# Second unit's token and query loads placed behind a GpSimd copy of the first scores' maxima

## The chip, the cores and the metric
The kernel runs on one core of a Trainium2 chip. The metric is device microseconds of one execution, as the median of three; a profile of one further execution shows what each engine did. The engines are PE (TensorE, matrix products), DVE (VectorE), ACT (ScalarE), POOL (GpSimd) and SP (SyncE). SP issues DMA transfers on the hardware queue q1, POOL issues them on the software queue q0; both are served by the same 16 DMA engines.

## The reference
One layer: RMSNorm, one input projection, two groups of four heads side by side, an output projection with a residual, then a mixture of experts with a residual. All inputs are float32, 2048 tokens of width 1024.

```python
h    = rms_norm(x)
proj = h @ w_in            # mLSTM q,k | v | o | i | f  and attention q | k | v
# group A, 4 heads: mLSTM memory; q, k through a causal conv of 4 taps and SiLU
b    = cumsum(log_sigmoid(f));  m_t = max(b + m, max_s(b_t - b_s + i_s))
hm   = (q k^T * exp(log_d - m_t)) v + exp(b + m - m_t) * q C,  divided by its norm
# group B, 4 heads, two 64-wide q/k maps c = 0, 1 each, q and k RMS-normed
p_c  = softmax(mask(q_c k_c^T / 8))          # chunk-causal, queries in blocks of 128
ha   = (p_0 - lambda * p_1) v
y    = x + concat(rms(sigmoid(o) * hm), rms(ha)) @ w_out
out  = y + moe(rms_norm(y))                  # top 1 of 4 groups, top 2 of 8 experts
```

The softmax subtracts the row's maximum; `nm` in the kernel is that maximum times -1/8, one column for each of the two maps.

## The kernel before
**Stages.** First the projection runs over pairs of 128-token blocks. It writes the normed tokens (`hT_d`), and attention's queries, keys and values (`q_d`, `k_d`, `v_d`), to DRAM; attention's q and k stand in two tiles `qkT` on the chip, from which the stores go out (L355). The group projected last holds the tokens that the next stage needs first. For these, eight loads (L348 on SP for queries, L349 on POOL for keys) copy q and k straight out of `qkT` into a tile `R`, without the way over DRAM.

Then come the heads, r = 0 to 3, each over 16 blocks g of 128 tokens; two blocks are a unit U of 256 tokens. For a unit the kernel needs its tokens `hs` (two loads of 1 MB from `hT_d`, L478; even units use `hs0`, odd ones `hs1`) and its queries `qt` (four loads of 128 KB, L487); for every four blocks it needs keys `kt` (L497, POOL) and values `va` (L499, SP). For unit 0 `hs0` is already on chip, and `qt` and part of `kt` are cast from `R` (L408, L409).

Of each block it computes: scores of both maps against all keys so far (L586, and L589 for the mask), their maxima `mx` (L590) and `nm` (L598), the exponential `prob` (L601, ACT), the combined probabilities (L618), their transposes (L632) and products with the values (L645); and of the mLSTM the values and output gate (vo, L94 to L96), the q and k of a unit (qk, L514 to L516, then the convolution at L531), a decay matrix `vb` (loaded at L671 from `vrow_d`, mask added on POOL at L672), and the products at L691 and L692.

**The passage between the two stages.** The gates of all tokens are computed once, in four pieces (lines 402 to 463): `gates_a` transposes the gate columns, casts `qt` and `kt` of unit 0 out of `R`, and runs two scans on DVE (`g_bc` at L420, `g_gm` at L421) over `g_lf`; `gates_b` transposes their last columns on PE (L427) and runs short scans in `g_mr` (L430 to L434); `gates_c` brings the result back through PE (L438) and makes `vrow`, which SP stores (L445); `gates_d` makes four tables. The pieces stand between the first block's matmuls, in this order of the program:

```python
load_kv(0); load_hs(1); load_qt(1)
gates_a(); vo_atoms(0); qk_atoms(0, 0); gates_b(); qk_atoms(0, 1)
gates_c(); score_atoms(0); vo_atoms(1); gates_d(0..3); combine_atoms(0)
```

**What sets the order.** The text of the program gives the work; a scheduler with estimates of its own orders the instructions of each engine and gives each tile its place in memory, taking up memory that earlier tiles have left. An instruction that writes such a place waits for those that read it before. Every engine, and each engine's DMA issues, run in their order, so an instruction that waits holds all behind it on that engine. `after(later, earlier)` keeps two instructions in order; `mark` holds instructions for it.

The lines below are those of the kernel before; in the changed kernel lines 495 to 740 stand 7 further down, so that L514 is L521 there.

Of the kernel before, what the change touches and what calls it, by code (L numbers as in the profile page):

```python
# [7 lines left out]
F32 = mybir.dt.float32  # L8
# [11 lines left out]
P = 128  # L20
# [40 lines left out]
def block_kernel(tc, a, out):  # L61
    nc = tc.nc
    V, A, G, T = nc.vector, nc.scalar, nc.gpsimd, nc.tensor
# [29 lines left out]
    def mm3(ps, xh, xl, wh, wl, start, stop):  # L93
        T.matmul(ps, xh, wh, start=start, stop=False)  # L94
        T.matmul(ps, xh, wl, start=False, stop=False)  # L95
        T.matmul(ps, xl, wh, start=False, stop=stop)  # L96
# [9 lines left out]
    with tc.tile_pool(name="const", bufs=1) as cp, tc.tile_pool(name="dram", bufs=1, space=DRAM) as dp:  # L106

        hT_d = dp.tile([NB, P, 2, DC, P], F32, name="hT_d")
        q_d = dp.tile([H, 4, 2, 2, 64, 512], F32, name="q_d")
# [47 lines left out]
        mark = {}  # L157

        def after(later, earlier):

            tc.add_manual_dep(later.ins, earlier.ins.name,
                              mybir.DependencyInfo(mybir.DependencyClass.NoSync, mybir.DependencyReason.DATA),
                              reason="issue order")
# [79 lines left out]
        with tc.tile_pool(name="wa", bufs=1) as wap, tc.tile_pool(name="sa", bufs=2) as sx, \  # L243
# [33 lines left out]
            with tc.tile_pool(name="wst", bufs=4, reuse_waits="tile") as sp:  # L277
                for j, (dst, src, n) in enumerate(pieces):
                    k = 2 if n > 4 else DC
                    for d in range(0, DC, k):  # L280
# [4 lines left out]
                        ld = nc.sync.dma_start(st, w_in[d * P:(d + k) * P, src:src + n].rearrange("(c p) n -> p c n", p=P))  # L285
# [9 lines left out]
            sp = sa2.__enter__()  # L295

            for p in range(NB):
                i, b = order[p], p % 2
# [83 lines left out]
        sp = rr.__enter__()  # L382
# [53 lines left out]
        def gates_c():  # L436
            pt = small(HC, 1)
            T.matmul(pt, gt["mp"], ones64[:1, :1], start=True, stop=True)  # L438
            mprev = g_tile("mprev", HC, 1)
            V.tensor_copy(mprev, pt)  # L440
            mt, ur, ir, em = gt["f"], gt["t1"], gt["lf"], gt["zr"]
            gt.update(ur=ur, ir=ir, em=em, dg=gt["gm"][:, :HC])
            V.scalar_tensor_tensor(mt, gt["bc"], mprev, gt["gm"], op0=OP.add, op1=OP.max)
            V.tensor_tensor(vrow, gt["bc"], mt, OP.subtract)
            nc.sync.dma_start(vrow_d, vrow)  # L445
            V.tensor_tensor(ur, gt["i"], gt["bc"], OP.subtract)
            A.activation(ir, vrow, AF.Exp, bias=mprev)
            V.tensor_scalar(em, mt, -1.0, math.log(4.0 * math.sqrt(128.0)), op0=OP.mult, op1=OP.add)
            A.activation(em, em, AF.Exp)
            V.tensor_scalar(gt["dg"], ident[:HC, :HC], ir[:, P - 1:P], None, op0=OP.mult)  # L450
# [14 lines left out]
        W, HS, QT, KT, VA, SIL, BLK, UN, CST = {}, {}, {}, {}, {}, {}, {}, {}, {}  # L465
        raw_prev = {}

        def w_of(r, k):
            j = r % 2 * 2 + k
            return (H4[j].rearrange("p (d n) -> p d n", d=DC), L4[j].rearrange("p (d n) -> p d n", d=DC))  # L470

        def load_hs(U):
            if U >= 32:
                return
            u = U % 8
            HS[U] = sp.tile([P, 2, 2, DC, P], F32R, name="hs1", bufs=1) if U % 2 else hs0
            for b in range(2):
                G.dma_start(HS[U][:, b], hT_d[2 * u + b])  # L478

        def load_qt(U):  # L480
            if U >= 32:
                return
            r, u = divmod(U, 8)
            QT[U] = sp.tile([P, 2, 2, 256], F32R, name="qt")
            for hl in range(2):
                for o in range(2):
                    G.dma_start(QT[U][hl * 64:(hl + 1) * 64, o],  # L487
                                q_d[r, u // 2, hl ^ o, :, :, u % 2 * 256:(u % 2 + 1) * 256].rearrange("m d t -> d m t"))

        def load_kv(B):  # L490
            if B >= 16:
                return
            r, sb = divmod(B, 4)
            KT[B] = sp.tile([P, 2, 512], F32R, name="kt", bufs=5)
            t0 = 0 if B else 256
            for hl in range(2):
                G.dma_start(KT[B][hl * 64:(hl + 1) * 64, :, t0:], k_d[r, sb, hl, :, :, t0:].rearrange("m d t -> d m t"))  # L497
            VA[B] = sp.tile([P, 4, HD], F32, name="va", bufs=5)
            nc.sync.dma_start(VA[B], v_d[sb * 512:(sb + 1) * 512, r * P:(r + 1) * P].rearrange("(b p) e -> p b e", p=P))  # L499
# [37 lines left out]
        def unit(U):  # L537
            if U not in UN:
                UN[U] = {n: sp.tile([P, 2, HD + x], F32, name=n) for n, x in (("mst", 0), ("ast", 0), ("num", 1), ("tho", 0))}
                UN[U]["nrm"] = sp.tile([P, 4], F32, name="nrm")  # L540
            return UN[U]

        def vo_atoms(g):
            r, i = divmod(g, NB)
            U, b = g // 2, g % 2
            box = {}

            def mms(d0):
                wh, wl = w_of(r, 1)
                if d0 == 0:  # L550
                    box["ps"] = pp.tile([P, 512], F32, name="w", bufs=3)
                ps = box["ps"][:, :256]
                for d in (d0, d0 + 1):
                    mm3(ps, HS[U][:, b, 0, d, :], HS[U][:, b, 1, d, :], wh[:, d, :], wl[:, d, :], d == 0, d == DC - 1)
                if d0 == DC - 2:
                    v1 = sp.tile([P, HD + 1], F32, name="v1")
                    G.memset(v1[:, HD:], 1.0)
                    v_ = A.activation(v1[:, :HD], ps[:, :HD], AF.Copy)
                    if g == 0:
                        after(v_, mark["LN"])  # L560
                    A.activation(unit(U)["tho"][:, b, :], ps[:, HD:], AF.Tanh, scale=0.5)
                    BLK.setdefault(g, {})["v1"] = v1
            return [lambda d0=d0: mms(d0) for d0 in (0, 2, 4, 6)]

        def score_atoms(g):
            r, i = divmod(g, NB)
            sb, b = divmod(i, 4)
            nch = sb + 1
            B = BLK.setdefault(g, {})
            width = [512 if c < sb else (b + 1) * P for c in range(nch)]  # L570

            def score(m, c):
                if m == 0 and c == 0:
                    B["mx"] = sp.tile([P, 2, 4], F32, name="mx")
                    B["nm"] = sp.tile([P, 2], F32, name="nm")
                    B["rs"] = sp.tile([P, 2, 4], F32, name="rs")
                    B["rt"] = sp.tile([P, 2], F32, name="rt")
                    B["rv"] = sp.tile([P, 2], F32, name="rv", bufs=3)
                    B["cc"] = sp.tile([P, 1], F32, name="cc")
                if c == 0:  # L580
                    B["p", m] = sp.tile([P, S], F32, name="prob", bufs=3)
                n = width[c]
                ps = pp.tile([P, 512], F32, name="sc", bufs=5)
                B["sc", m, c] = ps
                for o in range(2):
                    T.matmul(ps[:, :n], QT[g // 2][:, o, m, g % 2 * P:(g % 2 + 1) * P], KT[r * 4 + c][:, m, :n],  # L586
                             start=o == 0, stop=o == 1 and c < sb)
                if c == sb:
                    T.matmul(ps[:, n - P:n], qm, km, start=False, stop=True)  # L589
                V.reduce_max(B["mx"][:, m, c:c + 1], ps[:, :n], axis=AX.X)  # L590
                if c < nch - 1:
                    return
                mx, nm = B["mx"], B["nm"][:, m:m + 1]
                src = mx[:, m, 0:1]
                if nch > 1:
                    V.reduce_max(nm, mx[:, m, :nch], axis=AX.X)
                    src = nm
                V.tensor_scalar(nm, src, -0.125, None, op0=OP.mult)  # L598
                for c2 in range(nch):
                    n = width[c2]  # L600
                    mark["ACT"] = A.activation(B["p", m][:, c2 * 512:c2 * 512 + n], B["sc", m, c2][:, :n], AF.Exp, bias=nm,  # L601
                                 scale=0.125, accum_out=B["rs"][:, m, c2:c2 + 1])
            return [lambda m=m, c=c: score(m, c) for m in range(2) for c in range(nch)]
# [133 lines left out]
        HS[0] = hs0  # L737
        QT[0] = sp.tile([P, 2, 2, 256], F32R, name="qt")
        load_kv(0)
        load_hs(1)  # L740
        load_qt(1)
        def run(fs):
            for f in fs:
                f()
# [5 lines left out]
        run(qk_atoms(0, 1))  # L750
        gates_c()
        run(score_atoms(0))
        run(vo_atoms(1))
        for j in range(4):
            gates_d(j)
# [36 lines left out]
        for g in range(NS):  # L792
            r, i = divmod(g, NB)
            U = g // 2
# [84 lines left out]
        def first_half(e):  # L879

            return 12 * e - 4 if e else 0
# [301 lines left out]
        with tc.tile_pool(name="mo", bufs=2, reuse_waits="tile") as sp, \  # L1183
# [159 lines left out]
            for e in range(NE + 1):  # L1343
                u = first_half(e)
# [136 lines left out]
```

## Time and profile before

| | |
|---|---|
| median of 3 runs | 2171.48 us (2170.26 to 2174.47) |
| profiled execution | 2174.06 us, its span 2172.2 us |
| PE busy | 2046.9 us, 94% of the span |
| DVE / ACT / POOL busy | 1604.7 (74%) / 1231.4 (57%) / 516.6 (24%) us |
| DMA traffic | 449.79 MB, 207 GB/s over the span |
| mean granted clock of PE | 0.981 of full speed |

The projection ends at 327.5 us, the heads' stage starts there. Times in the rows are microseconds from the start of the span. A row of a timeline gives start, duration, engine, line, operation, the tile written and those read, and in brackets how long the engine idled before it and what ended that. [...] DMA rows give the size of one transfer and the time from issue to landing.

### The profile page before, as it was taken

The numbers are of one execution on the slowest core, as the hardware profiler recorded it, in microseconds if no ns is written. First come the engines' busy times: TensorE is split into PE (matmuls) and PEld (weight loads), VectorE is DVE, ScalarE is ACT, GpSimd is POOL, SyncE is SP. The second block draws the span as 40 slices with busy tenths as digits, with TensorE's granted clock in tenths as the row PEclk, the third lists the DMA queues.
The fourth block names the chain that finished last, engine by engine and source line by source line (L and its number), as shares of the span: only waits on it lengthen the run. The fifth ranks groups of instructions, "written<-read, shape, count | busy, mean of one in ns | idle before, by whom it ended". The sixth has DMA issues, their size and how long they took to land. (4 is left out here: it accounts for less than half of the span.)

```text
span 2172.2 us, 40513 instructions
## 1 busy us (share of the span) xinstructions
PE 2046.9 (94%) x13815; PEld 1734.3 (80%) x13816; DVE 1604.7 (74%) x4375; ACT 1231.4 (57%) x2820; POOL 516.6 (24%) x685
## 2 busy tenths in 40 slices
PE   7999997999999999999999999598999999999987
PEld 6888886899999899999987888476777666766765
DVE  7667655788687778878877777787878656786863
ACT  5344334666566566656663233477777656667764
POOL 4000003223322322232201111313232332223322
PEclk9999998999999999999999999799999999999999
DMA  7555438645663645375417844499999768898983
GB/s 231 177 173 171 160 102 249 167 123 134 190 159 107 175 140 159 89 200 162 122 51 258 271 146 137 145 330 303 363 348 347 243 228 295 301 334 285 352 280 75
DMA packets 241654, 449.79 MB, mean 207 GB/s; under 512 B 36432, under 2 KB 120720, under 8 KB 231376
## 3 DMA queue, kind: packets, MB, share of 16 engines
q1 hardware_dynamic: 192736, 317.08, 43.2%
q0 software_dynamic: 48352, 127.93, 21.6%
q8 instruction: 161, 2.64, 0.5%
q14 instruction: 133, 1.09, 0.2%
q10 hardware_dynamic: 272, 1.05, 0.1%
HBM read 377.72 MB, written 84.25 MB: 213 GB/s over the span
## 5 line engine op out<-in xcount | busy, mean ns | idle before, releaser
L70 DVE TENSOR_TENSOR L<-R,H 128x1024 fp32r<-128x1024 f32 x408 | 485.6, 1222 | 126.9 <-ACT H L66 117.1
L66 ACT ACTIVATE H<-R 128x1024 fp32r<-128x1024 f32 x408 | 415.8, 1056 | 30.7 <-DVE cnti L1174 9.2
L1247 PE MATMUL pgu<-H,xT 128*128 128x512 f32 x1024 | 359.9, 410 | 15.4 <-issue 6.6
L1247 PEld LDWEIGHTS pgu<-H,xT 128*128 128x128 f32 x1024 | 196.1, 191 | 58.0 <-issue 16.9
L601 ACT ACTIVATE prob<-sc,nm 128x512 f32<-128x512 f32 (+3 forms) x320 | 195.8, 623 | 50.8 <-DVE nm L598 44.4
L590 DVE TENSOR_REDUCE mx<-sc 128x1 f32<-128x512 f32 (+3 forms) x320 | 186.8, 602 | 24.2 <-PE sc L586 14.5
L1247 PE MATMUL pgu<-L,xT 128*128 128x512 f32 x512 | 203.2, 397 | 1.4 <-DVE L L70 1.4
L586 PE MATMUL sc<-kt,qt 128*128 128x512 f32 (+3 forms) x640 | 189.6, 386 | 2.0 <-ACT prob L601 1.8
L1262 PE MATMUL py<-H,hT 128*128 128x512 f32 x512 | 175.3, 405 | 11.0 <-issue 9.5
L94 PE MATMUL w<-H,hs 128*128 128x256 f32 x512 | 156.2, 305 | 5.8 <-DVE num L706 5.0
L645 PE MATMUL w<-va,aT 128*128 128x128 f32 x1088 | 155.6, 277 | 5.9 <-ACT raw L524 4.4
L514 PE MATMUL w<-hs,H 128*128 128x256 f32 x512 | 158.1, 309 | 1.7 <-ACT aT L636 0.9
L645 PEld LDWEIGHTS w<-va,aT 128*128 128x128 f32 x1088 | 139.3, 191 | 11.2 <-ACT raw L524 6.5
L515 PE MATMUL w<-hs,H 128*128 128x256 f32 x512 | 145.0, 283 | 0.0
L95 PE MATMUL w<-L,hs 128*128 128x256 f32 x512 | 145.0, 283 | 0.0
L516 PE MATMUL w<-hs,L 128*128 128x256 f32 x512 | 144.9, 283 | 0.0
L96 PE MATMUL w<-H,hs 128*128 128x256 f32 x512 | 144.9, 283 | 0.0
L1262 PEld LDWEIGHTS py<-H,hT 128*128 128x128 f32 x512 | 97.1, 190 | 43.7 <-issue 21.8
L1247 PEld LDWEIGHTS pgu<-L,xT 128*128 128x128 f32 x512 | 98.5, 192 | 18.3 <-DVE L L70 1.7
L1209 POOL DMA_INDIRECT xg<-h_d,ix x64 | 89.7, 1401 | 97.3 <-PE pt L1220 47.1
L1324 POOL TENSOR_SCALAR yE<-yE,ix 32x1024 f32<-32x1024 f32 (+1 forms) x20 | 57.0, 2852 | 231.4 <-ACT yE L1323 223.2
L1271 POOL DMA_INDIRECT out<-y,ix x32 | 57.5, 1795 | 226.5 <-ACT y L1267 125.4
(377 smaller groups left out, 5254.1 us busy)
## 6 DMA issues: line engine op xcount, KB each, us to landing
R<-w_gate SPq DMA_DIRECT2D x128, 512.0 KB, 10.8
R<-w_up SPq DMA_DIRECT2D x128, 512.0 KB, 11.9
R<-w_down SPq DMA_DIRECT2D x63, 1024.0 KB, 11.0
hs<-hT_d POOLq DMA_DIRECT2D x62, 1024.0 KB, 5.3
hT_d<-hs SPq DMA_DIRECT2D x16, 1024.0 KB, 4.0
qt<-q_d POOLq DMA_DIRECT2D x124, 128.0 KB, 6.3
xt<-x SPq DMA_DIRECT2D x30, 512.0 KB, 4.4
q_d<-qkT SPq DMA_DIRECT2D x32, 256.0 KB, 3.7
```

The lines of the kernel that those rows point to most:

```text
L66: return A.activation(dst, src, AF.Copy, scale=scale)
L70: return V.tensor_tensor(dst, src, h.bitcast(F32), OP.subtract)
L94: T.matmul(ps, xh, wh, start=start, stop=False)
L95: T.matmul(ps, xh, wl, start=False, stop=False)
L514: T.matmul(ps, l0, m0, start=d == 0, stop=False)
L515: T.matmul(ps, l0, m1, start=False, stop=False)
L586: T.matmul(ps[:, :n], QT[g // 2][:, o, m, g % 2 * P:(g % 2 + 1) * P], KT[r * 4 + c][:, m, :n], start=o == 0, stop=o == 1 and c < sb)
L590: V.reduce_max(B["mx"][:, m, c:c + 1], ps[:, :n], axis=AX.X)
L601: mark["ACT"] = A.activation(B["p", m][:, c2 * 512:c2 * 512 + n], B["sc", m, c2][:, :n], AF.Exp, bias=nm, scale=0.125, accum_out=B["rs"][: ...
L645: T.matmul(po, B["aT", c][:, kb * P:(kb + 1) * P], VA[r * 4 + c][:, kb, :], start=c == 0 and kb == 0, stop=c == nch - 1 and kb == nb[c] - 1)
L1247: T.matmul(pgu[c], xT[:, l, d, :], r[:, :, n], start=d == 0 and m == 0, stop=d == DC - 1 and m == 2)
L1262: T.matmul(py[n], hT[:, l, f, :], r[:, c], start=f == 0 and m == 0, stop=f == 3 and m == 2)
```

## The change
The two load calls of unit 1 move from ahead of `gates_a` to behind the first block's scores. A POOL copy of the first block's `nm` into a new tile `seen` (128x2) is added, and each of unit 1's six loads is ordered behind that copy; the loads of `hs0` for unit 2 are ordered behind the last of `hs1`. Nothing else is edited.

```diff
-        def load_hs(U):
+        def load_hs(U, behind=None):
 ...
             for b in range(2):
-                G.dma_start(HS[U][:, b], hT_d[2 * u + b])
+                ld = G.dma_start(HS[U][:, b], hT_d[2 * u + b])
+                if behind:
+                    after(ld, behind)
+                    mark["HS1"] = ld
+                elif U == 2:
+                    after(ld, mark["HS1"])
-        def load_qt(U):
+        def load_qt(U, behind=None):
 ...
+                    if behind:
+                        after(ld, behind)
 ...
         load_kv(0)
-        load_hs(1)
-        load_qt(1)
 ...
         run(score_atoms(0))
+
+        mark["POOL"] = G.tensor_copy(sp.tile([P, 2], F32, name="seen", bufs=1), BLK[0]["nm"])
+        load_hs(1, mark["POOL"])
+        load_qt(1, mark["POOL"])
```

The scheduler's answer is larger than the edit. On POOL, behind the loads into `R`, the order before is this (kt_3639 and kt_3873 are the keys of the first and second 512 tokens, hs1 and qt_3647 unit 1's tokens and queries; names in brackets are the queues and engines waited for):

```order
L497 DMA kt_3639<-k_d_62 64x2x256 [waits DMAHW3_49,DMAHW1_49,DMASW7_49]
L478 DMA hs1_3644<-hT_d_60 128x2048 [waits DMASW0_49]
L478 DMA hs1_3644<-hT_d_60 128x2048 [waits DMAHW6_49,DMASW1_49]
L487 DMA qt_3647<-q_d_61 64x2x256 [waits DMAHW6_49,DMASW2_49]
L487 DMA qt_3647<-q_d_61 64x2x256 [waits DMAHW7_49,DMASW3_49]
L487 DMA qt_3647<-q_d_61 64x2x256 [waits DMASW4_49]
L487 DMA qt_3647<-q_d_61 64x2x256 [waits DMASW5_49]
L557 MEMSET v1_3699 128x1
L557 MEMSET v1_3853 128x1
L497 DMA kt_3873<-k_d_62 64x2x512 [waits DMAHW2_49,DMAHW6_49,DMAHW0_49,DMASW6_49]
L497 DMA kt_3873<-k_d_62 64x2x512 [waits DMAHW3_49,DMAHW7_49,DMAHW1_49,DMASW7_49]
L672 TENSOR_TENSOR vb_3892<-vb_3892,cmask_78 128x128 [waits DMAHW4_49,PE_49]
```

And now, from the second load of kt_3639's successor on (kt_3875, kt_4406 and kt_5103 are the keys of the second to fourth 512 tokens):

```order
L564 MEMSET v1_3855 128x1
L504 DMA kt_3875<-k_d_62 64x2x512 [waits DMAHW2_49,DMAHW6_49,DMAHW0_49,DMASW0_49]
L504 DMA kt_3875<-k_d_62 64x2x512 [waits DMAHW3_49,DMAHW7_49,DMAHW1_49,DMASW1_49]
L504 DMA kt_4406<-k_d_62 64x2x512 [waits DMAHW2_49,DMAHW0_49,DMASW2_49]
L504 DMA kt_4406<-k_d_62 64x2x512 [waits DMAHW3_49,DMAHW1_49,DMASW3_49]
L504 DMA kt_5103<-k_d_62 64x2x512 [waits DMAHW5_49,DMAHW3_49,DMAHW6_49,DMAHW0_49,DMASW4_49]
L504 DMA kt_5103<-k_d_62 64x2x512 [waits DMAHW6_49,DMAHW4_49,DMAHW7_49,DMAHW1_49,DMASW5_49]
L759 COPY seen_3820<-nm_3799 128x2 [waits DMAHW4_49,DMAHW3_49,DMAHW5_49,DMAHW2_49,DVE_49]
L478 DMA hs1_3822<-hT_d_60 128x2048 [waits DMASW6_49,PE_49]
L478 DMA hs1_3822<-hT_d_60 128x2048 [waits DMASW7_49]
L492 DMA qt_3825<-q_d_61 64x2x256 [waits DMASW0_49]
L679 TENSOR_TENSOR vb_3894<-vb_3894,cmask_78 128x128 [waits DMAHW4_49]
```

Four loads of keys were pulled ahead of the copy, besides the two that stood there, and the copy waits for four hardware queue lanes as well as for DVE; these four are the last k_d stores. Tokens and queries of unit 1 come behind it, and behind them the first addition to `vb`.

On DVE at the start of the passage, behind the two copies L407, the order before:

```order
L409 CAST kt_3639<-R0_112 128x2x256 [waits DMASW4_49,DMASW5_49,DMASW3_49,DMASW2_49]
L418 MEMSET g_zr_3668 64x128
L521 MEMSET raw0_3733 128x3
L430 MEMSET g_mr_3751 1x68 [waits DMAHW4_49,DMAHW3_49,DMAHW5_49,DMAHW2_49,DMAHW6_49,DMAHW1_49,DMAHW7_49,DMAHW0_49,DVE_49]
L521 MEMSET raw1_3784 128x3
L416 SCALAR_TENSOR_TENSOR g_lf_3666<-g_f_3658,g_t1_3662 64x128 [waits DVE_49,Activation_49]
L420 SCALAR_TENSOR_TENSOR g_bc_3670<-g_lf_3666,g_zr_3668 64x128 [waits DVE_49]
L421 SCALAR_TENSOR_TENSOR g_gm_3671<-g_lf_3666,g_i_3654 64x128
```

And in the changed kernel, at the same place:

```order
L408 CAST qt_3638<-R0_112 128x1024 [waits DMAHW5_49,DMAHW6_49,DMAHW4_49,DMAHW3_49]
L409 CAST kt_3639<-R0_112 128x2x256 [waits DMASW4_49,DMASW5_49,DMASW3_49,DMASW2_49]
L418 MEMSET g_zr_3660 64x128
L416 SCALAR_TENSOR_TENSOR g_lf_3658<-g_f_3650,g_t1_3654 64x128 [waits DVE_49,Activation_49]
L528 MEMSET raw0_3725 128x3
L430 MEMSET g_mr_3743 1x68
L420 SCALAR_TENSOR_TENSOR g_bc_3662<-g_lf_3658,g_zr_3660 64x128 [waits DVE_49]
L421 SCALAR_TENSOR_TENSOR g_gm_3663<-g_lf_3658,g_i_3646 64x128
```

The cast of `qt` moved to the head, and the memset of `g_mr` has no DMA lane left among its waits.

On PE, ahead of the first product with hs1 (L514), the order before ends so, with the scores of unit 1's second block behind those of its first:

```order
L586 MATMUL sc_4113<-kt_3639,qt_3647 128x512 x2
L589 LDWEIGHTS qm_87
L589 MATMUL sc_4113<-km_90,qm_87 128x128
L586 MATMUL sc_4143<-kt_3639,qt_3647 128x512 x2
L589 LDWEIGHTS qm_87
L589 MATMUL sc_4143<-km_90,qm_87 128x128
L632 MATMUL w_3896<-ident_68,prob_3812 128x128
L678 MATMUL w_3910<-sil_3736 128x128
L679 MATMUL w_3910<-ident_68,sil_3736 128x128
L514 MATMUL w_3917<-hs1_3644,H0_113 128x256
```

In the changed kernel the scores of unit 0's second block (256 wide) stand there:

```order
L593 MATMUL sc_3903<-kt_3639,qt_3638 128x256
L596 LDWEIGHTS qm_87
L596 MATMUL sc_3903<-km_90,qm_87 128x128
L639 MATMUL w_3898<-ident_68,prob_3804 128x128
L685 MATMUL w_3912<-sil_3728 128x128
L686 MATMUL w_3912<-ident_68,sil_3728 128x128
L521 MATMUL w_3919<-hs1_3822,H0_113 128x256
```

The four groups of scores that read unit 1's queries (two of 384 and two of 512 columns) have moved behind this place.

## Rows read from the trace of the kernel before

**Rows 1.** Table of stages: PE, PEld, DVE, ACT, POOL busy; clock; DMA share; GB/s
```profile
330.40:341.80 11.40, 0.00 (x0) 0.00 (x0) 0.83 (x5) 0.00 (x0) 0.60 (x2) 0.50 1.10 339
341.80:347.50 5.70, 5.52 (x25) 5.20 (x26) 3.69 (x15) 0.42 (x1) 0.00 (x0) 0.50 1.03 316
...
356.00:390.00 34.00, 32.71 (x271) 31.90 (x270) 23.97 (x89) 19.77 (x66) 15.27 (x31) 1.00 0.83 228
1881.10:1886.90 5.80, 5.75 (x17) 4.03 (x21) 1.23 (x1) 1.22 (x2) 0.00 (x0) 0.50 0.02 6
```

**Rows 2.** Timeline of PE: start, duration, line, operation, idle time before
```profile
341.83 0.26 PE L427 MATMUL w<-ident,g_bc 64*1 64x64 f32 x1 [14.31 <-DVE g_bc L420]
...
347.72 0.27 PE L438 MATMUL w<-ones,g_mp 1*64 1x1 f32 x2
...
355.97 0.36 PE L514 MATMUL w<-hs,H 128*128 128x256 f32 x1
...
1881.15 0.80 PE L1262 MATMUL py<-H,hT 128*128 128x512 f32 x1 [4.08 <-issue]
```

**Rows 3.** Timeline of DVE in the passage
```profile
328.55 0.43 DVE L409 CAST kt<-R 128x512 fp32r<-128x512 f32 x1 [4.81 <-DMA R<-qkT]
...
340.94 0.12 DVE L430 MEMSET g_mr<- 1x68 f32 x1 [11.82 <-DMA k_d<-qkT]
...
341.04 0.28 DVE L416 SCALAR_TENSOR_TENSOR g_lf<-g_f,g_t 64x128 f32<-64x128 f32 x1
341.36 0.42 DVE L420 TENSOR_TENSOR_SCAN g_bc<-g_lf,g_zr 64x128 f32<-64x128 f32 x1
...
345.46 0.69 DVE L408 CAST qt<-R 128x1024 fp32r<-128x1024 f32 x1
...
351.30 0.21 DVE L598 TENSOR_SCALAR nm<-mx 128x1 f32<-128x1 f32 x2
```

**Rows 4.** Timeline of SP's DMA issues
```profile
325.78 3.33 SPq L355 DMA_DIRECT2D q_d<-qkT  x3
...
332.05 3.29 SPq L355 DMA_DIRECT2D k_d<-qkT  x1
335.45 10.22 SPq L499 DMA_DIRECT2D va<-v_d  x5
349.01 0.48 SPq L445 DMA_DIRECT2D vrow_d<-vrow  x1
```

**Rows 5.** DMA issues near 325, 328, 334, 290 and 355: KB each, us to landing
```profile
R<-qkT SPq DMA_DIRECT2D x1, 128.0 KB, 5.0
...
q_d<-qkT SPq DMA_DIRECT2D x1, 256.0 KB, 13.6
...
k_d<-qkT SPq DMA_DIRECT2D x1, 256.0 KB, 13.6
...
k_d<-qkT SPq DMA_DIRECT2D x4, 256.0 KB, 4.4
...
hs<-hT_d POOLq DMA_DIRECT2D x2, 1024.0 KB, 7.4
```

**Rows 6.** DMA queues from 330 to 336: packets, MB, share of 16 engines
```profile
q0 software_dynamic: 248, 1.80, 90.2%
q1 hardware_dynamic: 172, 0.17, 10.1%
```

**Rows 7.** The same from 286 to 297
```profile
q1 hardware_dynamic: 2238, 2.19, 78.6%
```

**Rows 8.** Timeline of POOL
```profile
37.85 0.18 POOL L359 COPY one<-vt 128x1 f32<-128x1 f32 x1 [2.71 <-ACT vt L329]
...
353.98 0.46 POOL L672 TENSOR_TENSOR vb<-vb,cmask 128x128 f32<-128x128 f32 x1 [22.70 <-DMA vb<-vrow_d]
354.58 1.12 POOL L478 DMA_DIRECT2D hs<-hT_d  x2
```

**Rows 9.** Groups of PE's instructions from 353.4 to 355.6: busy, mean ns
```profile
L586 PE MATMUL sc<-kt,qt 128*128 128x384 f32 (+1 forms) x8 | 2.2, 406 | 0.0
```

More of the change, by code (lines that the diff above doesn't have):

```diff
@@ L486, in load_qt @@
                 for o in range(2):
-                    G.dma_start(QT[U][hl * 64:(hl + 1) * 64, o],
-                                q_d[r, u // 2, hl ^ o, :, :, u % 2 * 256:(u % 2 + 1) * 256].rearrange("m d t -> d m t"))
+                    ld = G.dma_start(QT[U][hl * 64:(hl + 1) * 64, o],
+                                     q_d[r, u // 2, hl ^ o, :, :, u % 2 * 256:(u % 2 + 1) * 256].rearrange("m d t -> d m t"))
+                    if behind:
+                        after(ld, behind)
         def load_kv(B):
```

## The prediction
> **What bounds the kernel now.** I read the table of stages first, since the change touches one place: the passage from the projection to the first attention blocks. Away from it TensorE (PE) is the bound: from 356 to 390 us it works 32.71 of 34.00 us [rows 1]. The passage is the exception. From 330.40 to 341.80 PE does nothing while the DMA engines move 339 GB/s, and its granted clock is at 0.50; the 5.70 us behind that run at 0.50 too; from 356 on it is 1.00 [rows 1]. PE's own rows give the wait: 14.31 us until `g_bc` (L420) [rows 2]. The rows of VectorE (DVE) say why `g_bc` was late: after its wait of 4.81 us for the loads into `R` and one cast, DVE stood 11.82 us in front of a MEMSET of `g_mr` (1x68) [rows 3]. The trace names a k_d store as what ended that, but the last k_d store, issued at 332.05 with 13.6 us to landing, came down at 345.6 [rows 4, 5]. The last q_d store also took 13.6 us [rows 5]; issued at about 327.1, among the three of 325.78 [rows 4], it landed at 340.7, just ahead of the MEMSET at 340.94. The order agrees: this memset waits for every hardware DMA lane, as `g_mr` had been given memory that those stores and the R loads read.
>
> The stores are slow because POOL's queue carries 2 MB of `hs` and four `qt` loads at the same time. From 330 to 336 us that queue (q0) moved 248 packets with 1.80 MB and SP's (q1) 172 packets with 0.17 MB, 29 per us [rows 6]. Alone, SP's queue moved 2238 packets in 11 us, 203 per us [rows 7], and a k_d store took 4.4 us [rows 5].
>
> **The change, part by part.**
> *1. The long wait goes.* In the new order the memset of `g_mr` waits for nothing, since tiles got other places, and the cast of `qt` comes first. It waits for SP's four R loads; the last, issued at about 324.7, has 5.0 to landing: 329.7 [rows 5]. Behind that: cast of qt 0.69, of kt 0.43, memsets and `g_lf` 0.4, `g_bc` 0.42 [rows 3]: 331.7. PE restarts at 331.8 in place of 341.83, 10.0 us earlier. Bounds: R is not held up by the `kt` loads that now follow it on POOL's queue, or by 2 us.
>
> *2. The restart.* Before, PE's row L438 came 5.89 us behind L427 [rows 2], at half clock. Now PE idles 4.3 us and not 14.3. The nearest idle time is that of 4.08 us before 1881.15 [rows 2]; behind it 5.80 us ran at 0.50 [rows 1]. So I keep 5.9, and add 0.4 for the first scores, which now stand ahead of qk(0,1): L438 at 338.1. The other end is a restart at full clock: 24 matmuls at 0.125 us a step (271 in the 34.00 us at 1.00) and not at 0.228 (25 in the 5.70 us at 0.50) [rows 1], 2.5 us earlier.
>
> *3. The new wait.* hs1 is issued behind the copy `seen`. That needs the second `nm`, which ended at 351.5, 3.8 us behind L438 [rows 2, 3]: now 341.9, and a small POOL copy of 0.18 [rows 8] makes 342.1. It waits for the last four k_d stores too, because `seen` lies in memory that they read. POOL's queue now carries 1.75 MB of kt (two loads of 128 KB, six of 256) from about 327.6; with 0.75 MB of q_d beside it at 339 GB/s [rows 1] that is done at 335.0. Say that none of the 1 MB of k_d has moved by then: about 1050 packets at 203 per us take 5.2 us, and it lands at 340.2. So `nm` decides, by 1.9 us. The first matmul on hs1 reads both halves; the second is issued 0.56 behind the first and lands 7.4 later [rows 5, 8]: 350.1. Before, PE began hs1 at 355.97 [rows 2]: **-5.87**.
>
> Behind the copy on POOL stand hs1, four qt, the first mask-add of `vb` and hs0's loads. That add ran at 353.98 [rows 8], vrow_d having been issued at 349.01 [rows 4], 4.97 us. vrow is now ready by about 340, but SP has five va loads to issue ahead of it (10.22 us, to 345.67 [rows 4]; less where the queue is emptier), so vb is added between 346 and 350.7, and 1 to 3 us later if its packets meet hs1's. Who waits is L691, whose `kw` needs vb: it stands behind hs1's first 18 matmuls, at about 354.5. I cost it at 0, and at +1.5 where that cover is gone.
>
> *4. Work that moves behind the wait.* Four groups of scores (384 and 512 wide) stood ahead of hs1's first matmul, from 353.4 to 355.6, and fill these 2.2 us [rows 9]. They read unit 1's queries, which now come late, so they go behind: **+2.2**, as PE has no slack there.
>
> *5. A second idle time.* PE has done what stands ahead of hs1 by about 343.8 (353.4 less the 9.6 by which L438 is earlier), waits for the first probabilities until about 346 and for hs1 until 350.1: 4 to 6 us. By the case at 1881 the clock falls again, and 24 of hs1's matmuls take 0.103 us more each: **+2.5** (bounds: 0, if it doesn't fall, and 2.9, half of 5.80).
>
> [...]
>
> *Sum*: -5.87 + 2.2 + 2.5 = -1.2 us. The profiled execution took 2174.06 us, 1.9 over its span, and so would take 2172.9; it lies 2.58 above the median of 2171.48, from which I forecast **2170.3 us**. The rest of the program keeps its instructions, and PE is 96% busy from 356 to 390 [rows 1], so a shift there reaches the end.
>
> **Rivals.** (a) *Faster: the short waits cost no clock.* With the second one free, -5.87 + 2.2 = -3.7. With the first free too, L438 is at 335.6 and `nm` at 339.4; then hs1 goes out at 339.6 to 340.2 (k_d) and lands at 347.6 to 348.2: -5.6 to -6.2 in all. For it: 10 us of PE's wait do go. Against it: the half clock behind the 4.08 us.
>
> (b) *Slower: the copy waits for the stores.* If k_d still takes 13.6 us, because 1.5 MB of kt takes turns with it as hs did, it lands at 345.6 and hs1 at 353.6: 2.4 won, 2.2 gone to the scores and 2.5 to the clock, +2.3; with vb late behind hs1 as well, +3.8. It decides from k_d landing later than 342.1, and is a loss from 343.3 on. For it: 172 packets beside 248 [rows 6]. Against: kt has fewer bytes than hs and qt had, in smaller packets, and ends earlier.
>
> (c) *It does not do what it says.* The kt loads hold R up by 2 us; everything behind follows, hs1 lands at 352.1, and the sum is +0.8.
>
> (d) *vb behind hs1.* hs1's large packets alternate with the small ones of vrow and vb, L691 waits 1.5 us for kw, and the sum is +0.3. [...]
>
> **How the numbers follow.** Forecast 0.45, (a) 0.28, (b) 0.14, (c) 0.05, (d) 0.08. A measurement of this kernel tells about 0.2% (4.3 us) from no change. The forecast, (c) and (d) lie within that, and so does the half of (a) that ends at -3.7. Beyond it: 0.14 from (a), and 0.09 from the forecast where R and hs1 land sooner than beside today's transfers; faster 0.23. Slower by more than that takes (b) with more than I priced, or a new wait further on, where the order differs up to the sixth block: 0.15. The range runs from (a)'s -6.2 to (b)'s +3.8: 2165.2 to 2175.3.
>
> **What would show it.** Right: PE's wait at L427 near 4 us and its end at about 331.8; `seen` released by DVE and not by a DMA, at about 342; a second wait of PE of some 4 us at its first matmul on hs1, ended by hs1's load near 350; the clock at 0.50 behind both. Wrong: `seen` after 343 behind a k_d store (b); R landing after 331 (c); no 0.50 behind the second wait (a); PE waiting at L691 for `kw` (d); or idle time further on that wasn't there.

## The result and the profile after

The changed kernel takes 2186.26 us (median of 4 runs, 2182.77 to 2189.28); beside it the kernel before took 2171.98 us on the same chip. The ratio is 1.0064, 95% interval 1.0043 to 1.0085: slower by 14 us, outside the predicted range. The profiled execution took 2183.98 us with a span of 2182.2, 10.0 more than before.

**The passage's steps came about as forecast; what they are worth in time is not shown.** Table of stages of the changed kernel, columns as in [rows 1]: busy time of each engine with its count of instructions in brackets, the granted clock of PE as a share of full speed, the share of busy DMA engines, and GB/s:

```profile
327.50:330.40 2.90, 0.00 (x0) 0.00 (x0) 1.79 (x8) 0.08 (x1) 1.24 (x3) 0.69 1.04 261
330.40:336.20 5.80, 5.64 (x28) 5.24 (x28) 3.12 (x15) 0.42 (x1) 0.00 (x0) 0.57 1.17 360
336.20:343.10 6.90, 5.96 (x46) 5.21 (x45) 5.22 (x26) 4.16 (x14) 2.72 (x6) 1.00 1.02 305
350.70:356.50 5.80, 5.78 (x29) 5.80 (x30) 0.65 (x3) 1.54 (x5) 4.64 (x10) 0.55 0.78 235
356.50:390.00 33.50, 32.94 (x270) 31.25 (x269) 25.90 (x93) 20.99 (x71) 10.59 (x22) 1.00 0.68 187
```

The 14.31 us wait of [rows 2] is two waits now, and behind each the clock stands near 0.5 (0.57 and 0.55) for 5.8 us. PE's timeline of the changed kernel, only rows with idle time before them:

```profile
330.42 0.26 PE L427 MATMUL w<-ident,g_bc 64*1 64x64 f32 x1 [4.02 <-DVE g_bc L420]
341.01 0.27 PE L456 MATMUL w<-ident,g_lf 64*128 64x64 f32 x1 [0.16 <-DVE ucol L461]
342.67 0.33 PE L639 MATMUL w<-ident,prob 128*128 128x128 f32 x1 [0.78 <-DVE nm L605]
350.72 0.55 PE L521 MATMUL w<-hs,H 128*128 128x256 f32 x1 [7.38 <-DMA hs<-hT_d]
```

POOL's timeline of the changed kernel, the copy and what follows it (compare [rows 8]):

```profile
340.06 0.19 POOL L759 COPY seen<-nm 128x2 f32<-128x2 f32 x1 [11.33 <-DMA k_d<-qkT]
340.57 1.15 POOL L478 DMA_DIRECT2D hs<-hT_d  x2 [0.32 <-issue]
341.69 2.43 POOL L492 DMA_DIRECT2D qt<-q_d  x4
351.22 0.45 POOL L679 TENSOR_TENSOR vb<-vb,cmask 128x128 f32<-128x128 f32 x1 [7.11 <-DMA vb<-vrow_d]
```

I compare the two traces by the start times of instructions that both have. Ahead of the passage the changed kernel already runs 1.1 us earlier, a difference of pace between two executions. At 400 us it is 2.6 us earlier, so by these two traces the passage gave 1.5 us, and 1.2 was forecast. Such a number scatters by more than itself. The three other kernels below that only add a small edit to the changed one (experiments 4, 8 and 6) give 1.8, 0.9 and -1.4 us over the same stretch, and the four with the passage of before (5, 10, 9 and 1) give 1.5, 0.4, -0.1 and -0.5. And 1.1 us of the 1.5 is a wait further on, in PE's timeline of the kernel before, that the changed kernel doesn't have:

```profile
388.14 0.66 PE L632 MATMUL w<-ident,prob 128*128 128x128 f32 x4 [1.09 <-ACT tho L561]
```

**The loss comes a thousand microseconds later.** The lead is 3.4 us at 1300. Then it is lost in steps in the experts' stage, which the diff doesn't touch: the changed kernel is still 0.9 us early at 1550, 1.0 late at 1600, 3.7 at 1800 and 9.9 at 2100. One group of waits shows there that is not among the longer ones before. ACT's waits from 1390 to the end, first in the changed kernel, then before (total, times, longest):

```profile
ACT H L66 <- issue: 27.7, 6, 5.3
```
```profile
ACT H L66 <- issue: 2.8, 3, 1.2
```

"issue" says that nothing the profile knows of was waited for; five of the six stops told of below are in the 27.7 us. Here is the first of the six places, ACT's timeline in the changed kernel and the same place before:

```profile
1431.73 0.74 ACT L1236 ACTIVATE th<-pgu 128x256 f32<-128x256 f32 x2
1437.39 4.85 ACT L66 ACTIVATE H<-R 128x1024 fp32r<-128x1024 f32 x5 [4.92 <-DMA R<-w_down]
```
```profile
1436.34 0.74 ACT L1227 ACTIVATE th<-pgu 128x256 f32<-128x256 f32 x2
1437.29 2.96 ACT L66 ACTIVATE H<-R 128x1024 fp32r<-128x1024 f32 x3 [0.20 <-ACT th L1227]
```

For this one of the six the profile names a weight load as the releaser. But between the two rows stands a compare-and-branch (L1395, L1386 before; not counted as busy), and the time is lost there: if an expert has at most 128 tokens, the engine jumps over a block of some sixty instructions. In the trace's branch records ACT's next instruction of any kind, waits on semaphores included, comes 0.37 us behind it before, and 5.09 us behind it now. Five more such stops of 5.29 to 5.47 us stand at 1545.5, 1654.0, 1803.3, 1926.6 and 2050.1, at every fifth expert (2, 7, 12, 17, 22, 27); before, these branches cost 0.37 us each. A smaller one of 2.36 us stands behind ACT's last branch (L1441; 0.38 before), at 2169; by then the changed kernel is 9.9 us late already, and 10.0 at the end.

What a stop does downstream is seen in DVE's and then PE's rows of the changed kernel:

```profile
1438.54 5.77 DVE L70 TENSOR_TENSOR L<-R,H 128x1024 fp32r<-128x1024 f32 x5 [3.59 <-DMA R<-w_down]
```
```profile
1444.70 0.66 PE L1229 MATMUL pt<-ident,xg 128*128 128x128 f32 x4 [1.27 <-DVE hT L70]
```

ACT's casts of weights (`H`) come late, DVE takes the five remainders (`L`) in a row, and the `hT` that PE needs stands behind these. PE's waits from 1390 on, the changed kernel and before:

```profile
PE pt L1229 <- DVE hT L70: 8.2, 6, 2.0
```
```profile
PE pt L1220 <- DVE hT L70: 2.1, 1, 2.1
```

So the six stops' 32 us cost PE much less, since it has other products to do: its idle time in this stage, summed over its records, is 51.9 us and was 41.5.

**What differs there.** In the built programs, order, waits and addresses of the experts' stage are the same in both kernels, but ACT's code ahead of it is 1800 instructions long and was 1797. (The trace has 2299 records of ACT ahead of the first branch and had 2296, since it lists the sum that an activation can return as a record of its own; the difference is the same.) The three are instructions that only wait on a semaphore. They stand at the first square into `h2`, in the norm behind the heads (L990, L981 before), which waits now for DMASW 3, 6, 2, 7, 1 and 0 besides DMAHW6 and DVE. By the built programs the change made the scheduler lay `hs1` at byte 179584 (before: 130112) of each partition; it ends at 195968 and so overlaps by 320 bytes with `h2` at 195648, and the square has to wait for the loads that filled `hs1`. Experiment 4 agrees: with `hs1` 512 bytes lower, the three waits are gone from this square. The waits take no time where they stand: ACT is idle for 4.60 us ahead of this square in both kernels, by DVE. They only take places in the code.

### The profile page after: what moved, and what is told of

Read it like the earlier page. It is cut to its first block, busy times and chain, and to the rows that moved or that the text cites. A ratio compares the mean times of both kernels' runs of the same rounds, so it can differ in the third digit from the quotient of the medians.

```text
span 2182.2 us, 40520 instructions
## 1 busy us (share of the span) xinstructions
PE 2049.9 (94%) x13815; PEld 1734.1 (79%) x13816; DVE 1603.9 (73%) x4375; ACT 1228.7 (56%) x2820; POOL 529.1 (24%) x686
## 5 line engine op out<-in xcount | busy, mean ns | idle before, releaser
L1280 POOL DMA_INDIRECT out<-y,ix x32 | 68.6, 2144 | 241.4 <-ACT y L1276 128.8
## 6 DMA issues: line engine op xcount, KB each, us to landing
R<-w_up SPq DMA_DIRECT2D x128, 512.0 KB, 11.5
```

## The experiments

Ratios are to runs of the kernel before on the same chip, with 95% intervals. "ACT's length" is the number of ACT's instructions in front of the experts' stage in the built program, "DVE's" the same for DVE. The texts ahead of each run name times by the 2172 us of the kernel before; on the chips of these runs it took 2176.8 to 2177.9, so their differences to it, and not their times, are to be compared.

**1. Only the length.** To the kernel before, loads where they were:

```diff
         V.memset(ones64, 1.0)
+        for _ in range(3):
+            A.activation(ones64[:, :1], ones64[:, :1], AF.Copy)
```

> The kernel before, with three more tiny ScalarE copies (64x1) at its start, so that ScalarE's code of the experts' stage lies three instructions further on, as it does in the changed kernel (there through three wait-only instructions ahead of the norm at L981). Nothing in the passage changes. Theory (place of ScalarE's code): six stops of about 5.3 us on ScalarE behind the branch of L1386 in the experts' stage, as in the changed kernel, and the time goes up by 11 to 15 us, to 2183 to 2187. Rival (the experts' stage is slower because it starts some us earlier and meets its weight loads in another phase, or because of where the heads' tiles lie): no such stops, 2172 +- 2.

1.0040 [1.0023, 1.0057]; six stops of 5.22 to 5.30 us behind the same six branches. The first, ACT's timeline:

```profile
1434.43 0.75 ACT L1229 ACTIVATE th<-pgu 128x256 f32<-128x256 f32 x2
1440.27 1.06 ACT L66 ACTIVATE H<-R 128x1024 fp32r<-128x1024 f32 x1 [5.09 <-issue]
```

The slowdown appears without the change. It is 8 to 9 us here, less than the 11 to 15 that the text said and than the changed kernel's 14; experiment 9, another way to the same length, gives 13.

**2. The change without the length.** To the changed kernel, tiles declared early, in an order that lays `hs1` below `prob`:

```diff
+        for nm in ("i", "f", "t1", "lf", "zr", "bc", "gm"):
+            sp.tile([HC, P], F32, name="g_" + nm, bufs=1)
...
+        sp.tile([P, 2, 2, DC, P], F32R, name="hs1", bufs=1)
```

> The changed kernel with hs1 given memory ahead of the probabilities' tiles, so that no tile of the output stage meets its loads: ScalarE's code in front of the experts has as many instructions as in the kernel before. The gate behind the copy stays. Theory (place of code): no stops on ScalarE in the experts' stage; what the passage wins reaches the end, 2166 to 2171 (2172 less 1 to 5). Rival (earlier start or the gate itself costs it): still 2183 to 2188.

0.9991 [0.9979, 1.0004]; ACT's length is 1797 and there is no stop. PE in the passage:

```profile
328.78 0.26 PE L427 MATMUL w<-ident,g_bc 64*1 64x64 f32 x1 [5.09 <-DVE g_bc L420]
341.49 0.33 PE L639 MATMUL w<-ident,prob 128*128 128x128 f32 x1 [0.82 <-DVE nm L605]
347.53 0.55 PE L521 MATMUL w<-hs,H 128*128 128x256 f32 x1 [5.24 <-DMA hs<-hT_d]
```

By start times this trace gained 2.0 us over the passage, and nothing was lost from 1300 to 2100. The text's 1 to 5 us fit the ratio, but so does nothing at all: the change as it was meant is worth 0.2% at most.

**3. Only the false wait of `g_mr` removed.** The kernel before, with the loads in their old places and other places in memory by the same means (18 kinds of tiles declared early, `raw`, `g_mr` and `prob` among them).

> The kernel before, its loads in their old places, with only the order of the heads' tiles in memory changed, so that g_mr, the convolution's buffers and the first probabilities no longer lie in memory that the last q_d and k_d stores read. ScalarE's code is one instruction shorter than before. Theory (the 11.8 us stop of VectorE was a matter of memory alone, and moving the loads was not needed for it): VectorE does not stop at g_mr, PE's wait at L427 falls from 14.3 to 4 to 5 us, hs1 is there in time (by 340), no second wait of 7 us; 2162 to 2168. Rival (the two megabytes of hs1 in the queue are what holds the passage up, whatever the layout): R's or the stores' landings still set it, PE waits 10 us or more in all, 2169 to 2172.

0.9994 [0.9976, 1.0012]. The win of 5 to 10 us didn't come; by start times the passage gave 1.0 us, within the scatter. PE starts at 326.25, but by the trace ACT's first exponential then waits for a k_d store, as `prob` now takes memory that this store reads, and PE behind it. ACT, then PE:

```profile
342.19 0.37 ACT L601 ACTIVATE prob<-sc,nm 128x128 f32<-128x128 f32 x1 [7.56 <-DMA k_d<-qkT]
```
```profile
326.25 0.21 PE L427 MATMUL w<-ident,g_bc 64*1 64x64 f32 x1 [2.32 <-DVE g_bc L420]
...
342.70 1.01 PE L586 MATMUL sc<-kt,qt 128*128 128x384 f32 x2 [4.08 <-ACT prob L601]
351.38 0.80 PE L645 MATMUL w<-va,aT 128*128 128x128 f32 x2 [2.67 <-ACT aT L636]
```

One false wait went and the next on the same stores took its place.

**4. and 5. Lengths between.** The changed kernel with `g_er` in another pool (512 bytes less below `hs1`; ACT's length 1799), and the kernel before with one activation as in 1 (1798).

```diff
-            er = sp.tile([1, 2, HC], F32, name="g_er", bufs=1)
+            er = c1.tile([1, 2, HC], F32, name="g_er")
```

> The changed kernel with one small tile (g_er, 512 bytes) in another pool, so that hs1 lies 512 bytes lower and the norm at L981 no longer waits for its loads; another instruction of the same stage does now, and ScalarE's code is one instruction shorter than in the changed kernel, two longer than before. The order of all work is the same. Theory (place of code): the six stops are either all there at full size or all gone, as the branch's target lies on one or the other side of a border of the fetched code: 2183 to 2188, or 2166 to 2171, and nothing between. Rival (phase of the loads): 2183 to 2188 and no relation to the stops.

> The kernel before with one one-column ScalarE activation in its first microseconds, so that ScalarE's code in front of the experts' stage is 1798 instructions long (1797 before, 1799 and 1800 in the two kernels that stop five and six times). Theory, code place: the border lies between 1797 and 1800 and moves by expert. If 1798 is still on the good side, no stop over 1 us behind the branch L1388 and the time of before within 0.2%; if it is on the bad side, up to six stops of 5.1 to 5.5 us and +7 to +13 us. Rival, memory: the stops came from what else the other kernels change; then none here. A number of stops between two and five with +2 us for each would show that each stop has its own border.

1.0042 [1.0025, 1.0060] and 1.0039 [1.0019, 1.0060], with five stops each, at the same experts but the first (2). The text of 4 had this wrong: not all six come together. That of 5 left it open and fits, with 8 to 9 us in the +7 to +13 that it named. Five stops cost as much as six within the intervals. The border for five of them lies between 1797 and 1798, one instruction, and that for expert 2 between 1799 and 1800. ACT's timeline of 5, at expert 2 and at expert 7:

```profile
1434.94 4.86 ACT L66 ACTIVATE H<-R 128x1024 fp32r<-128x1024 f32 x5 [0.21 <-ACT th L1229]
...
1543.47 0.75 ACT L1229 ACTIVATE th<-pgu 128x256 f32<-128x256 f32 x2
1549.36 2.01 ACT L66 ACTIVATE H<-R 128x1024 fp32r<-128x1024 f32 x2 [5.14 <-issue]
```

**6. Eight more.** The changed kernel with nine activations as in 1 (1808, as one wait fewer was needed).

> The changed kernel with nine one-column ScalarE activations in its first microseconds: ScalarE's code in front of the experts' stage is 1808 instructions long (in the changed kernel the count is 1800). Theory, code place: whether a stop comes hangs on where each branch and its target lie, so another eight instructions can take the stops away (then 2170 to 2174 us, as the kernel with 1797) or move them to other experts; the six experts 2, 7, 12, 17, 22, 27 with unchanged stops of 5.1 to 5.5 us would say that 8 instructions are too few to leave the bad stretch. Rival, length alone (more instructions in front, more stops): all six stay or more come, 2184 us or over.

1.0043 [1.0026, 1.0061], five stops of 5.01 to 5.45 us, expert 2 without one. Eight instructions more take one stop away and leave five. This tells the two theories poorly apart.

**7. The copy earlier.** Experiment 2, with the copy reading the maxima:

```diff
-        mark["POOL"] = G.tensor_copy(sp.tile([P, 2], F32, name="seen", bufs=1), BLK[0]["nm"])
+        mark["POOL"] = G.tensor_copy(sp.tile([P, 2], F32, name="seen", bufs=1), BLK[0]["mx"][:, :, 0])
```

> The changed kernel with the memory order of the second experiment (hs1 below prob, ScalarE's code 1797 long, no stop expected), and the GpSimd copy reads the row maxima mx in place of their scaled negatives nm. The copy waits for the second maximum, which is done 2.1 to 2.4 us ahead of nm's second column (336.4 against 338.7 in that experiment), so the eight loads start about 2.2 us earlier. Theory: TensorE's wait for hs at L521 falls from 5.2 to about 3 us if the loads take as long as before, and the time is 1.5 to 2.5 us below the second experiment's, 0.2 to 0.3% under before. Rival: the k load's last stores and the v loads are still on the queues then and hs takes longer, or releases the copy itself at k_d; then the wait stays over 4.5 us and the time within 0.2% of before.

0.9993 [0.9979, 1.0006]. The rival came nearly true: k_d releases the copy, and PE's wait only falls to 4.47 (it said over 4.5, the theory about 3). POOL, then PE:

```profile
337.38 0.58 POOL L779 COPY seen<-mx 128x2 f32<-128x2 f32 x1 [10.18 <-DMA k_d<-qkT]
338.14 1.15 POOL L478 DMA_DIRECT2D hs<-hT_d  x2 [0.18 <-DMA k_d<-qkT]
```
```profile
349.61 0.55 PE L521 MATMUL w<-hs,H 128*128 128x256 f32 x1 [4.47 <-DMA hs<-hT_d]
```

Behind this wait PE stands another 1.68 us for `kw` at L698, a wait of the kind that the prediction's rival (d) put at 1.5 us, seen in this kernel alone. No version here beats the kernel before by more than its runs can tell.

**8. The branch hint earlier.** The changed kernel (1800) with each expert's hint two of eight parts earlier:

```diff
-                        if d == 3:
+                        if d == 1:
                             tc.mark_branch_hint_location(f"more{e}", n > P, engines)
```

> The changed kernel with the branch hint of each expert (L1376) given two of eight parts earlier (d == 1 in place of d == 3); ScalarE's count in front of the stage stays 1800. In the changed kernel the hint is 5.9 us ahead of the branch at 1432 and the stop ends 11.1 us behind the hint. Theory A, the target's code is on its way and late: with some 4 to 5 us more of warning the stops shrink to under 1.5 us or go, and the time falls to 2170 to 2176 us. Theory B, what is fetched does not hold the target, whenever it is asked for: the six stops stay at 5.1 to 5.5 us and the time at 2182 to 2186 us. A hint that comes earlier moves the branch's place among the instructions not at all, so theory B expects the same six experts.

1.0029 [1.0016, 1.0043]; the hint now comes 9.1 to 11.5 us ahead of these six branches, and the six stops stay at 5.02 to 5.31 us. The stops stayed, as theory B expected; what is fetched for a branch is not shown. The ratio is lower than the changed kernel's 1.0064, and the intervals only touch at 1.0043, so whether the earlier hint gave back time elsewhere stays open.

**9. and 10. ACT's length or DVE's.** In all stopped kernels so far DVE's length, too, had risen, from 3901 to 3902 up to 3905. Two more kernels, both from before, part them: five squares near the stage (ACT 1800, DVE 3901), and three memsets at the start (ACT 1797, DVE 3904).

```diff
                 A.activation(R["h2"], x2, AF.Square, accum_out=R["ss"])
+                if i == 1:
+                    for _ in range(5):
+                        A.activation(R["h2"][:, :1], x2[:, :1], AF.Square)
```
```diff
         V.memset(ones64, 1.0)
+        for _ in range(3):
+            V.memset(ones64[:, :1], 1.0)
```

> The kernel before with five one-column ScalarE squares behind one block's square at L981, near the experts' stage and 1000 us away from the passage. ScalarE's code in front of the stage is 1800 instructions long (two waits go, five squares come); VectorE's is 3901 and GpSimd's 868, as before. In all kernels so far that stop, VectorE's count was raised too (3902 to 3905 for 3901), so that is a rival. Theory, ScalarE's code place: five or six stops of 5.0 to 5.5 us behind the branch at L1386 (moved by three lines), ratio to before 1.003 to 1.006. Rival, VectorE's code place: its count is that of before, so no stop and a ratio within 0.2% of 1.

> The kernel before with three one-column VectorE memsets in its first microseconds. VectorE's code in front of the experts' stage is 3904 instructions long, the count of the two padded kernels that stop (there with ScalarE at 1798 and 1800); ScalarE's stays at 1797. Theory, ScalarE's code place: no ScalarE stop over 1.2 us behind the branch, ratio within 0.2% of 1. Rival, VectorE's code place: five or six ScalarE stops of 5 us and 1.003 to 1.006.

1.0060 [1.0043, 1.0077] with six stops of 5.14 to 5.39 us for the squares; 0.9988 [0.9973, 1.0004] with none for the memsets. ACT's timelines, 9 and then 10:

```profile
1435.08 0.74 ACT L1230 ACTIVATE th<-pgu 128x256 f32<-128x256 f32 x2
1440.91 2.96 ACT L66 ACTIVATE H<-R 128x1024 fp32r<-128x1024 f32 x3 [5.09 <-DMA R<-w_down]
```
```profile
1433.13 0.75 ACT L1229 ACTIVATE th<-pgu 128x256 f32<-128x256 f32 x2
1434.08 4.86 ACT L66 ACTIVATE H<-R 128x1024 fp32r<-128x1024 f32 x5 [0.20 <-ACT th L1229]
```

Over all kernels: ACT's length 1796 (experiment 3) and 1797 (before, 2, 7, 10): no stop; 1798, 1799 and 1808: five; 1800 (changed kernel, 1, 8, 9): six. DVE's length has no part in it. Nor have those of POOL and SP: in 9, with stops, POOL's is that of the kernel before, and SP's is that of 3, without. ACT's last branch goes with them: 2.36 to 2.52 us in every kernel that stops, 0.38 in the others.

## Why the prediction was wrong

- *Step 1, the long wait goes:* right. `g_mr` has no wait, PE restarts at 330.42 (said: 331.8).
- *Step 2, the restart at half clock:* right. L438 comes at 336.24, 5.82 behind L427 (said 6.3 with the scores ahead of it), with the clock at 0.57.
- *Step 3, the new wait:* near. The copy ran at 340.06 (said 342.1). The last k_d store released it, 0.8 us behind the second `nm`, and not `nm`; the store's landing at about 340 was as estimated (340.2). hs1's second load then took about 9.5 us and not 7.4; PE began hs1 at 350.72 (said 350.1). In experiment 2, where `nm` does release the copy (338.74), it took about 7.5 us, so what held it here is not shown.
- `vb` (rival d) was added at 351.22 and L691, now L698, came at 355.12 with no wait for it. Its packets did not alternate with hs1's, as (d) supposed: from 344 to 348 POOL's queue moved 219 packets and SP's one, though vb's loads were issued from 344.72 on. In the kernel before, from 333 to 339, the two queues had moved 589 and 590.
- *Steps 4 and 5:* right in kind. The second wait was 7.38 us (said 4 to 6), since PE came to it earlier; the clock fell behind it, to 0.55.
- *The sum for the passage* of -1.2 met -1.5 in the trace, but that is luck in part: 1.1 us of it is the wait at 388, of which the sum knew nothing, and the kernels with this order of loads lie between -2.0 (experiment 2) and +1.4 (experiment 6).
- **The step that failed is the last one of the sum**: "The rest of the program keeps its instructions, and PE is 96% busy from 356 to 390 [rows 1], so a shift there reaches the end." The shift did last to 1300. But the rest does not keep its instructions: three waits came to ACT's code, from a new overlap in memory 320 bytes wide. That put ACT's branches at other places of the code, and six jumps cost 5.1 to 5.5 us each in place of 0.37. From 1300 to the end this trace lost 13 us; the six other kernels that stop lost 10.5 to 13.4 over the same stretch of theirs, and the four others that don't between -2.0 and 5.3. No rival held it: the order was weighed only "up to the sixth block", though the signs of being wrong named "idle time further on that wasn't there", which is what came.
- The chance of 0.15 for slower was too small for a change after which the scheduler lays out memory anew.

What stays open is why a place stops. Instruction packets appear among the DMA queues: in the 5.1 us of the first stop (1432.2 to 1437.3) of the changed kernel, and in the 5.1 us behind the same branch before, the rows are the same:

```profile
q8 instruction: 1, 0.02, 1.2%
q14 instruction: 1, 0.01, 0.4%
```

Up to 1390 us of the kernel before, queue q8 has 72 packets of 16 KB, and PE has taken some 18,400 instructions with its weight loads and waits, about 256 for each packet; from these counts I take q8's packets for PE's, which is an estimate. The packet to look at is that of q14, of 8 KB. In each of the 39 stops of ACT of 5 us in the seven kernels that have them, a packet of q14 starts 3.4 to 3.8 us behind the branch and ends 1.25 to 1.58 us before ACT's next instruction. Behind the same six branches of the kernel before, one starts 3.5 to 4.2 us behind the branch too, while ACT runs on after 0.37. An ACT that waits at a stop for its code to come in, and has that code already where it doesn't stop, would fit these times, but this is the author's guess: that the packet is ACT's is not shown, as its records don't name an engine. Nor is it shown why one instruction more ahead of a branch decides, or why it is the same single instruction (1798 in place of 1797) for five branches that lie five experts' code apart.

## What to carry to other kernels

An edit that makes a scheduler lay out memory anew can change the time at a place that it doesn't touch: compare the counts of instructions per engine ahead of every stage with branches (here ACT's went from 1797 to 1800, and six stops of 5.1 to 5.5 us came), and not only the order around the edit. Where a profile shows idle time "issue" right behind a compare-and-branch, shift that engine's code by a few instructions before looking for a data dependence (here one more brought five such stops, experiment 5). Where a wait on reused memory is removed, look which other tile lies on the same memory: here `g_mr`, `prob` and `seen` each waited for the last stores out of `qkT` in turn.

## What the runs showed of the hardware

- Behind each of its 68 branches in the kernel before, ACT's next instruction came within 0.4 us; in the changed kernel it came 5.09 to 5.47 us behind six of them and 2.36 behind the last, and in all seven kernels that stop, 5.0 to 5.5 us behind five or six. At five branches one instruction more ahead of them decided (1797 against 1798). Each of these 39 stops of 5 us ended 1.25 to 1.58 us after an 8 KB packet of queue q14, which the profile calls "instruction", had come in. DVE has such stops in every kernel here, unmoved by three more instructions (experiment 10): 5.7 to 6.4 us at one expert (6.21 in the kernel before, 6.16 in the changed one) and 7.1 us at two others.
- In the trace, waits on semaphores are instructions of their own: three of them, 307 records of ACT ahead of the first branch that stops, came with a loss of 13 us, one or three activations of one column with 8 to 9 us (experiments 5 and 1), and five with 13 (experiment 9).
- A hint 9.1 to 11.5 us ahead of the branch, in place of 5.9, left the stops as they were (5.02 to 5.31 us).
- In the changed kernel, PE's idle times of 4.02 and 7.38 us were each followed by 5.8 us at about half of the full clock (0.57 and 0.55).
